# Stick-breaking q, k and half of v by seven-product block pairs, the residual spilled in the meantime, low parts of weights in the raw tile's bytes

## The chip, the cores and the metric

One Trainium2 chip, and one of its cores. The time is that of one execution on the device, in microseconds (us); the kernel before takes 2441.69 us (median of 3 runs, 2441.59 to 2443.45). The engines are TensorE (PE: matmuls, and PEld: its weight loads), VectorE (DVE), ScalarE (ACT), GpSimd (POOL) and SyncE (SP, whose queue issues the weight loads here).

## The reference

Two layers of a decoder over 256 positions of width 2048, in float32. Layer 0 runs state-space heads and latent attention side by side, layer 1 is stick-breaking attention; a SwiGLU FFN of width 5632 follows each. The part that the change is about:

```python
def stick_breaking_mixer(h, w_qkv, w_out):
    qkv = (h @ w_qkv).reshape(bsz, seq, 3, SB_HEADS, SB_HEAD_DIM)
    q, k, v = qkv[:, :, 0], qkv[:, :, 1], qkv[:, :, 2]
    for i in range(seq // Q_BLOCK):
        z = jnp.einsum('bqhd,bkhd->bhqk', q[:, q0:q1], k[:, :q1]).astype(jnp.float32) * scale
        log_keep = jnp.where(mask, -jax.nn.softplus(z), 0.0)
        later = lax.cumsum(log_keep, axis=log_keep.ndim - 1, reverse=True) - log_keep
        weight = jnp.where(mask, jnp.exp(jax.nn.log_sigmoid(z) + later), 0.0)
        outs.append(jnp.einsum('bhqk,bkhd->bqhd', weight.astype(v.dtype), v[:, :q1]))
    return jnp.concatenate(outs, axis=1).reshape(bsz, seq, SB_WIDTH) @ w_out

x = x + mix                                         # after each mixer
x = x + swiglu_ffn(rms_norm(x, ffn_norm[layer]), w_gate[layer], w_up[layer], w_down[layer])
```

There are 16 heads of 128; q, k and v have 2048 columns each.

## The kernel before

**Exact enough products.** A float32 weight tile (128 x 4 x 512, 1 MB, so 512 rows of the matrix by 512 columns) is loaded by SP's queue, cast by ACT to a rounded high part `wh` (line 271), and DVE subtracts it from the raw tile to get the low part `wl` (line 272). Activations are parted likewise. A product takes three matmuls of 512 columns for each 128 rows of K and each 128 positions: high by high, high by low, low by high.

**Two ways to project.** `project` (lines 371 to 373) does that for all 16 steps of K and both halves of the positions: 96 matmuls for one block of 512 columns. `pair` (line 585) does two blocks of 512 columns at once. Over the first 1024 rows of K it sees operand and weights as 2 x 2 blocks and computes the 2 x 2 product with seven block products (M1 to M7, 12 matmuls each) in place of eight; the second 1024 rows are done plainly (c0 to c3, 24 matmuls each): 180 matmuls. For that, DVE forms four differences of weight tiles (line 547; two into `wsum` tiles, one for M4, one over b12) and seven operand tiles (`operand_ready`). Four PSUM banks hold the sums. M1's, M5's, M6's and M7's state of a bank is copied by ACT as it stands after them (line 604, `kept`), and DVE adds the copy to another bank when that is done. `p2` and `p4` (the left block) are done with c2, `z` and `p3` (the right block) with c3. The tables `HALF` and `LATE` give the order of the eleven pieces; `LATE` is used for the first pair of an output projection, whose later operand blocks are not there yet.

**Where each is used.** Gate and up in both FFNs (22 pairs) and the three output projections (6 pairs) go by `pair`, all else by `project`, q, k and v of the stick layer among it.

**Stick layer** (`stick`). For each of four groups of four heads: project q, project k, scale both on leaving PSUM, transpose them on PE, then `stick_weights` (scores, mask on POOL, Abs and Exp on ACT for four heads; then Ln for four heads, the maximum step on DVE, a split; then the running sums by a triangular matmul and an Exp), then project v and `stick_out` (weights by v). The residual stays in the SBUF tile `xres` all along.

**What sets the order.** PE's order is the order of the code: tasks (`spawn`) advance at `tick`s, which stand every 4 to 8 matmuls. The other engines are in-order queues, which a scheduler fills by priority: weights (`wprio`) first, `urgent` ahead of them. Raw tiles have 4 buffers, `wh` and `wl` 3 each, `wsum` 2.

Of the kernel before, what the change touches and what calls it, by code (L numbers as in the profile page):

```python
# [8 lines left out]
F32 = mybir.dt.float32  # L9
# [17 lines left out]

class Trunk:
# [6 lines left out]
    def __init__(self, ctx, tc, ins, out):  # L35
# [4 lines left out]
        self.wp = ec(tc.tile_pool(name="weights", bufs=4))  # L40
# [4 lines left out]
        self.dp = ec(tc.tile_pool(name="scratch", bufs=1, space=bass.MemoryType.DRAM))  # L45
        self.shared = None
        self.region("acts")
        ctx.callback(self.region, None)
        self.banks = ["acc0", "acc1", "acc2", "acc3"]
        self.n = self.parts = 0  # L50
        self.pressing = []
        self.now, self.tasks = 0, []
# [23 lines left out]
    def after_urgent(self):  # L76
        order = ExitStack()
        for part, ins in self.pressing:
            if part <= self.parts - 3:
                order.enter_context(self.tc.issue_after(ins))  # L80
        self.pressing = [p for p in self.pressing if p[0] > self.parts - 3]
        return order
# [28 lines left out]
    def region(self, kind):  # L111

        if self.shared is not None:
            self.shared.__exit__(None, None, None)
        self.shared = None
        if kind:
            self.shared = self.tc.tile_pool(name=f"shared_{kind}", bufs=2, reuse_waits="tile")
            self.xp = self.shared.__enter__()

    def s2x(self, shape, dt=F32):  # L120

        return self.xp.tile([P, *shape], dt, name=self.nm("s2x"), tag="s2x", bufs=8)

    def wsum(self):
        return self.xp.tile([P, 4, 512], F32, name=self.nm("wsum"), tag="wsum", bufs=2)

    def wtile(self, tag="w", dt=F32, bufs=4):
        return self.wp.tile([P, 4, 512], dt, name=self.nm(tag), tag=tag, bufs=bufs)

    def part(self, tag):  # L130

        return self.wtile(tag, F32R, 3)
# [24 lines left out]
    FILL = 16  # L157


    def constants(self):  # L160
        nc, i = self.nc, self.i
        c = lambda shape, name, dt=F32: self.cp.tile(shape, dt, name=name)
        self.xres = c([P, 2, D], "xres")

        nc.gpsimd.memset(c([P, self.FILL], "fill"), 0.0)
# [103 lines left out]
    def split(self, hi, lo, src):  # L269
        nc = self.nc  # L270
        nc.scalar.copy(hi, src)  # L271
        return nc.vector.tensor_tensor(lo, src, hi.bitcast(F32), op=ALU.subtract).ins  # L272
# [57 lines left out]
    def load_split(self, view, nk, n):  # L330

        nc = self.nc
        for k0 in range(0, nk, 4):
            k1 = min(nk, k0 + 4)
            res = []
            with self.priority(self.wprio):
                self.wprio += 1000
                w = self.wtile()
                for dst, src in view(w, k0, k1):
                    nc.sync.dma_start(dst, src)  # L340
# [4 lines left out]
                wh, wl = self.part("wh"), self.part("wl")  # L345
                step = 1 if self.wprio < 102000 else 2 if self.wprio < 106000 else k1 - k0
                for c in range(0, k1 - k0, step):
                    d = c + step
                    self.last_split = self.split(wh[:, c:d, :n], wl[:, c:d, :n], w[:, c:d, :n])
                for k in range(k0, k1):  # L350
                    res.append((wh[:, k - k0, :n], wl[:, k - k0, :n]))
# [12 lines left out]
    def project(self, xT, view, nk, n=512, done=None, stagger=0):  # L364
# [4 lines left out]
        def unit(k, t, hi, lo, wh, wl):  # L369
            ts = slice(t * P, (t + 1) * P)  # L370
            nc.tensor.matmul(ps[t], hi[:, ts], wh, start=k == 0, stop=False)  # L371
            nc.tensor.matmul(ps[t], hi[:, ts], wl, start=False, stop=False)  # L372
# [31 lines left out]
    def norm_block(self, st, j, g, wait=2, rank=None):  # L404
# [3 lines left out]
        def gen():  # L408
            yield from self.transpose_split(
                lambda t, k: x[:, t, j * 512 + k * P:j * 512 + (k + 1) * P], res, g[:, 4 * j:4 * j + 4], wait, rank)  # L410
            for t in range(2):
                self.square_sum(x[:, t, j * 512:(j + 1) * 512], st["ssq"][:, t, j:j + 1])
        st["xT"].append((self.spawn(gen()), res))

# [19 lines left out]

    def add_tile(self, t, c, j, scale=None):
# [11 lines left out]
    def project_residual(self, st, view, scale=None, done=None):  # L447
# [3 lines left out]
        def add(n):  # L451
            def take(t, c, s):
                nc.vector.tensor_tensor(s, c, s, op=ALU.add)
# [74 lines left out]
    def wload(self, view, k0):  # L528
        w = self.wtile()
        with self.priority(self.wprio):  # L530
            self.wprio += 100
            for dst, src in view(w, k0, k0 + 4):
                self.nc.sync.dma_start(dst, src)
        return w

    def wsplit(self, w):
        wh, wl = self.part("wh"), self.part("wl")
        self.parts += 1
        with self.priority(self.wprio), self.after_urgent():
            self.wprio += 100  # L540
            self.last_split = self.split(wh, wl, w)
        return wh, wl

    def wsub(self, o, p, q):
        with self.priority(self.wprio):
            self.wprio += 100
            self.nc.vector.tensor_tensor(o, p, q, op=ALU.subtract)  # L547
# [3 lines left out]
    HALF = ("M1", "M5", "c0", "M3", "M6", "M2", "M7", "M4", "c1", "c2", "c3")  # L551

    LATE = ("M1", "M5", "M2", "M3", "M6", "M4", "M7", "c0", "c1", "c2", "c3")

    def pair(self, st, va, vb, left, right, order=HALF):
# [8 lines left out]
        for m in ("b11", "b12", "c0", "b22", "b21", "c1", "c2", "c3") if order is self.HALF else (  # L564
                "b11", "b12", "b22", "b21", "c0", "c1", "c2", "c3"):
            v = (va, vb)[int(m[2]) - 1 if m[0] == "b" else int(m[1]) % 2]
            raw[m] = self.wload(v, 4 * int(m[1]) - 4 if m[0] == "b" else 8 + int(m[1]) // 2 * 4)
        b11, b12, b22, b21 = (raw[m] for m in ("b11", "b12", "b22", "b21"))
        src = {"M1": b11, "M3": b22, "M2": b21, "M7": b12, **raw}
        t1, t2 = (self.wsum() for _ in range(2))  # L570
        src["M5"], src["M6"] = t1, t2
        self.join(st["xT"][0][0])
        self.join(st["xT"][1][0])
        if "paced" in st:
# [9 lines left out]
        def mm(b, x, y, stop=False):  # L584
            nc.tensor.matmul(ps[b], x, y, start=b not in started, stop=stop, skip_group_check=True)  # L585
            started.add(b)

        def add(b, x, w, keep=None):

            wh, wl = w  # L590
# [6 lines left out]
            for k, (hi, lo) in enumerate(x):  # L597
                mm(b, hi, wl[:, k], stop=k == n - 1)
# [15 lines left out]
        ops = lambda m: [(st["S"][place[m]][0][:, k], st["S"][place[m]][1][:, k]) for k in range(4)]  # L614
        for m in order:
            if m == "M1":
                self.wsub(t1, b12, b11)
            if m == order[2]:
                self.wsub(t2, b22, t1)
            if m == order[3]:  # L620
# [618 lines left out]
```

## Time and profile before

| | |
|---|---|
| median of 3 runs | 2441.69 us |
| the profiled execution | 2440.8 us, of which 2439.1 are the span |
| granted TensorE clock, mean | 0.999 |
| from HBM | 450.85 MB, 186 GB/s over the span |
| weight splits, wl from w (line 272) | 431, 966.8 us on DVE |
| casts, wh from w (line 271) | 431, 804.8 us on ACT |
| matmuls of `pair`, high and low parts | 3360 and 1680 |
| matmuls of `project`, each of three lines | 1600 |

The span runs from 0. The first layer's input projections end near 322 us, its output projections near 660, its FFN near 1338; q, k, v and the attention of the stick layer take from there to 1636; the second FFN starts near 1730. A row of a timeline or of the chain gives start and duration; a group gives instructions, busy time and mean ns of one, then the idle time ahead of them and what ended it.

### The profile page before, as it was taken

To read this page: it belongs to the slowest core of one execution; us is meant where nothing else is said; L and a number is where in the kernel's file an instruction comes from. 1 tells how busy PE (TensorE), PEld (TensorE's weight loads), DVE (VectorE), ACT (ScalarE), POOL (GpSimd) and SP (SyncE) were. 2 spreads that over 40 slices of the span, in tenths; PEclk is the share of its full clock that TensorE was granted. 3 is DMA by queue.
4 is the path that set the end of the run, shared out by engine and by line. 5 is a ranking of instruction groups with operands and counts; after the bars stand their busy time and mean duration, and the time that the engine had idled before them with its cause. 6 is when DMAs were issued, how large, how long until landed. Compare 5 with 4: busy or idle time off the path is not lost.

```text
span 2439.1 us, 27764 instructions
## 1 busy us (share of the span) xinstructions
PE 2406.7 (99%) x11104; PEld 1983.4 (81%) x11104; DVE 1815.6 (74%) x1533; ACT 1348.3 (55%) x1337; POOL 159.8 (7%) x210
## 2 busy tenths in 40 slices
PE   8999999999999999999999999999999999999998
PEld 7788888777788888888888888878788888888887
DVE  6776597578998777777775445559998777777775
ACT  6665565555755555555554556556665555555553
POOL 1341111110000000000000000000000000000001
PEclk9999999999999999999999999999999999999999
DMA  8654556424565666666665555545665566666663
GB/s 276 190 184 149 186 190 181 130 87 159 197 213 198 216 216 216 209 205 215 201 213 182 181 173 162 167 138 191 205 208 199 201 213 216 216 216 204 210 222 115
DMA packets 261377, 466.38 MB, mean 191 GB/s; under 512 B 21436, under 2 KB 46144, under 8 KB 261248
## 3 DMA queue, kind: packets, MB, share of 16 engines
q1 hardware_dynamic: 255168, 446.48, 55.1%
q0 software_dynamic: 5504, 17.09, 1.9%
q8 instruction: 87, 1.43, 0.2%
q10 hardware_dynamic: 576, 1.05, 0.1%
q14 instruction: 42, 0.34, 0.0%
HBM read 450.85 MB, written 2.13 MB: 186 GB/s over the span
## 4 chain that ended last, share of the span: by engine, by line
PE 77%; issue 14%; DVE 5%; ACT 2%; DMA 1%; POOL 1%; POOLq 0%; SPq 0%; DVEq 0%; ACTq 0%
PE acc L585 42%; PE acc L371 10%; PE acc L373 10%; PE acc L372 10%; DVE wl L272 2%; ACT wh L271 1%; DVE wsum L547 1%; DMA w<-in_w_out_even_dram 1%; PE at L1161 1%; POOL s L797 1%; PE at L1084 1%; PE tr L277 1%; PE at L1160 0%; PE tr L279 0%; DVE s L272 0%
## 5 line engine op out<-in xcount | busy, mean ns | idle before, releaser
L272 DVE TENSOR_TENSOR wl<-w,wh 128x2048 fp32r<-128x2048 f32 (+2 forms) x431 | 966.8, 2254 | 350.4 <-ACT wh L271 349.9
L271 ACT CAST wh<-w 128x2048 fp32r<-128x2048 f32 (+2 forms) x431 | 804.8, 1876 | 513.1 <-PE acc L373 244.8
L585 PE MATMUL acc<-wh,s 128*128 128x512 f32 x3360 | 838.2, 391 | 7.0 <-ACT wh L271 4.4
L585 PEld LDWEIGHTS acc<-wh,s 128*128 128x128 f32 x3360 | 627.1, 188 | 138.0 <-ACT wh L271 5.4
L371 PE MATMUL acc<-wh,s 128*128 128x512 f32 (+1 forms) x1600 | 639.2, 400 | 0.6 <-ACT wh L271 0.6
L373 PE MATMUL acc<-wh,s 128*128 128x512 f32 (+1 forms) x1600 | 621.7, 389 | 0.0
L372 PE MATMUL acc<-wl,s 128*128 128x512 f32 (+1 forms) x1600 | 620.4, 388 | 0.2 <-DVE wl L272 0.2
L585 PE MATMUL acc<-wl,s 128*128 128x512 f32 x1680 | 450.6, 390 | 4.6 <-DVE wl L272 4.6
L585 PEld LDWEIGHTS acc<-wl,s 128*128 128x128 f32 x1680 | 314.6, 188 | 73.8 <-DVE wl L272 8.7
L373 PEld LDWEIGHTS acc<-wh,s 128*128 128x128 f32 x1600 | 300.7, 188 | 63.3
L372 PEld LDWEIGHTS acc<-wl,s 128*128 128x128 f32 x1600 | 301.4, 188 | 58.0 <-issue 1.9
L371 PEld LDWEIGHTS acc<-wh,s 128*128 128x128 f32 x1600 | 301.1, 188 | 57.8 <-issue 1.9
L272 DVE TENSOR_TENSOR wl<-wsum,wh 128x2048 fp32r<-128x2048 f32 x84 | 192.0, 2287 | 43.8 <-ACT wh L271 42.7
L271 ACT CAST wh<-wsum 128x2048 fp32r<-128x2048 f32 x84 | 160.6, 1914 | 92.6 <-PE acc L373 60.3
L547 DVE TENSOR_TENSOR wsum<-w,wsum 128x2048 f32<-128x2048 f32 x56 | 129.1, 2306 | 4.7 <-DMA w<-in_w_out_even_dram 3.3
L604 ACT COPY s<-acc 128x512 f32<-128x512 f32 x112 | 65.8, 588 | 100.0 <-PE acc L585 100.0
L653 POOL DMA_DIRECT2D s<-s x44 | 23.7, 539 | 1471.4 <-DVE s L650 1405.8
L645 ACT ACTIVATE s<-s,rstd 128x512 f32<-128x512 f32 x44 | 31.9, 724 | 94.6 <-DVE s L644 94.6
L547 DVE TENSOR_TENSOR wsum<-w,w 128x2048 f32<-128x2048 f32 x28 | 65.0, 2320 | 24.0 <-DMA w<-in_w_up_dram 21.5
L547 DVE TENSOR_TENSOR w<-w,w 128x2048 f32<-128x2048 f32 x28 | 64.1, 2290 | 0.0
L326 ACT ACTIVATE s<-acc,rstd 128x512 f32<-128x512 f32 x48 | 32.2, 688 | 49.2 <-PE acc L373 47.9
L649 DVE TENSOR_TENSOR s<-acc,s 128x512 f32<-128x512 f32 x44 | 30.2, 687 | 36.5 <-PE acc L585 36.5
(230 smaller groups left out, 1281.3 us busy)
## 6 DMA issues: line engine op xcount, KB each, us to landing
w<-in_w_gate_dram SPq DMA_DIRECT2D x88, 1024.0 KB, 5.3
w<-in_w_up_dram SPq DMA_DIRECT2D x88, 1024.0 KB, 5.1
w<-in_w_down_dram SPq DMA_DIRECT2D x88, 1024.0 KB, 5.2
w<-in_w_qkv_dram SPq DMA_DIRECT2D x48, 1024.0 KB, 5.1
w<-in_w_in_dram SPq DMA_DIRECT2D x47, 1024.0 KB, 5.1
w<-in_w_out_even_dram SPq DMA_DIRECT2D x32, 1024.0 KB, 5.0
w<-in_w_out_odd_dram SPq DMA_DIRECT2D x16, 1024.0 KB, 4.9
s<-s POOLq DMA_DIRECT2D x44, 256.0 KB, 4.0
```

The source lines that it names most:

```text
L271: nc.scalar.copy(hi, src)
L272: return nc.vector.tensor_tensor(lo, src, hi.bitcast(F32), op=ALU.subtract).ins
L277: self.nc.tensor.transpose(out.bitcast(F32R), src, self.ident_r)
L326: self.nc.scalar.activation(o, ps[t], func, scale=scale[:, t:t + 1])
L371: nc.tensor.matmul(ps[t], hi[:, ts], wh, start=k == 0, stop=False)
L372: nc.tensor.matmul(ps[t], hi[:, ts], wl, start=False, stop=False)
L373: nc.tensor.matmul(ps[t], lo[:, ts], wh, start=False, stop=k == nk - 1)
L547: self.nc.vector.tensor_tensor(o, p, q, op=ALU.subtract)
L585: nc.tensor.matmul(ps[b], x, y, start=b not in started, stop=stop, skip_group_check=True)
L604: self.kept = nc.scalar.copy(o, ps[b]).ins
L645: nc.scalar.activation(s, s, AF.Silu, scale=rstd[:, t:t + 1])
L649: nc.vector.tensor_tensor(s, c, s, op=ALU.add)
```

## The change

**Stick layer.** For each group, q's and k's block of 512 columns become the two blocks of one `pair`; v of groups 0 and 1 is one more pair after group 1; v of groups 2 and 3 are two plain projections at the end. The first FFN now ends by making the operand sums for these pairs (`operand_sums`: 12 sums and 4 splits; M1, M2 and M4 take plain operands). The sums for the output projection are made late (`operand_late`). In `stick_weights` the splits are urgent and the triangular matmuls interleave with them.

**Memory.** `xres` is a fixed region now. It is written to DRAM by POOL's queue as the first FFN ends and comes back before the odd output projection; its bytes hold the scores `z` (`spare`) meanwhile. In layer 0 they hold the state-space head's `xdt`, and x is loaded anew before the even output projection. The low part is written over the raw tile: 6 slots that hold raw and low part, 2 for sums, 3 high parts and from the even output projection on 4. A load into a slot waits for the last matmul of the low part that was there.

**Orders.** `HALF` has M4 ahead of M7 and c2 ahead of c1; `LATE` has M3 and M6 ahead of M2. The difference for M4 is made at M6. Tiles are loaded three ahead, the others when their piece is reached.

```diff
-        self.wp = ec(tc.tile_pool(name="weights", bufs=4))
+        self.weight_slots()
+    HIGH, LOW, SUMS = 4, 6, 2
+    def wtile(self, tag="w"):
+        slot = min((s for s in self.slots[tag] if s.left == 0), key=lambda s: s.time)
+        slot.readers, slot.left = [], -1
+        return slot
+    def filled(self, slot, *writers):
+        if slot.last is not None:
+            for ins in writers:
+                self.tc.add_manual_dep(ins, slot.last.name, mybir.DependencyInfo(
+                    mybir.DependencyClass.Sync, mybir.DependencyReason.DATA), reason="the low part's last product")
...
-    def wsplit(self, w):
-        wh, wl = self.part("wh"), self.part("wl")
+    def wsplit(self, w, uses):
+        wh, wl = self.high(), w.part
...
-    HALF = ("M1", "M5", "c0", "M3", "M6", "M2", "M7", "M4", "c1", "c2", "c3")
-    LATE = ("M1", "M5", "M2", "M3", "M6", "M4", "M7", "c0", "c1", "c2", "c3")
+    HALF = ("M1", "M5", "c0", "M3", "M6", "M2", "M4", "M7", "c2", "c1", "c3")
+    LATE = ("M1", "M5", "M3", "M6", "M2", "M7", "M4", "c0", "c1", "c2", "c3")
...
-            if m == "M4":
+            if m == "M6":
+                load("b21")
+                b21 = src["M2"] = raw["b21"]
                 src["M4"] = self.wsum()
                 self.wsub(src["M4"], b21, t2)
...
-            self.norm_block(nst, n, gain_next)
+            self.norm_block(nst, n, gain_next, blocks=True, spill=self.saved, pause=4)
...
         for g in range(4):
-            qk = []
-            for part in range(2):
-                ps = self.project(xT, self.cols(wq, part * 2048 + g * 512), KD)
-                rstd = rstd or self.norm_end(st)
-                raw = self.evac(ps, AF.Copy, rstd)
+            raw = [[None, None], [None, None]]
+            self.pair(st, cols(0, g), cols(1, g), take(raw[0]), take(raw[1]))
+            qk, wts = [], []
+            for r in raw:
                 res = []
...
+            weights.append((self.spawn(self.stick_weights(qk, wts, g & 1)), wts))
+            if g in (0, 2):
+                continue
+            v = [[None, None], [None, None]]
+            if g == 3:
+                oT["late"] = self.spawn(self.operand_late(oT, 2))
+            if g == 3:
+                v = [self.evac(self.project(self.pairs(st["xT"]), cols(2, n), KD), AF.Copy, st["rstd"]) for n in (2, 3)]
+            else:
+                self.pair(st, cols(2, g - 1), cols(2, g), take(v[0]), take(v[1]))
...
+        oT["residual"] = self.spawn(self.residual_late(oT))
...
-            z, e = self.s2([N]), self.s2([N])
+            z, e = self.spare[4 * half + h][:, :N], self.s2([N])
...
+        self.slots["wh"] += self.more_high
         self.project_residual(uT, lambda n: self.cols(wo, n * 512), lambda: r_u)
```

**PE, the start of the stick layer.** Before, group 0's q projection takes high, low and high matmuls by turns for both halves of the positions (`acc_9921`, `acc_9922`), with the operand `s` and the weight parts `wh` and `wl`:

```order
L371 MATMUL acc_9921<-wh_9925,s_1675_9586 128x512
L372 MATMUL acc_9921<-wl_9926,s_1675_9586 128x512
L373 MATMUL acc_9921<-wh_9925,s_1676_9587 128x512
L371 MATMUL acc_9922<-wh_9925,s_1675_9586 128x512
L372 MATMUL acc_9922<-wl_9926,s_1675_9586 128x512
L373 MATMUL acc_9922<-wh_9925,s_1676_9587 128x512
```

Now the end of M1 (bank `acc_9160`), a transpose for the operand's third block, and the start of M5 (`acc_9161`). The low part is `w_69`, the raw tile's own bytes:

```order
L681 MATMUL acc_9160<-wh_66,s_875_8824 128x512
L681 MATMUL acc_9160<-wh_66,s_876_8825 128x512
L681 MATMUL acc_9160<-w_69,s_872_8807 128x512 x2
L681 MATMUL acc_9160<-w_69,s_875_8824 128x512 x2
L318 MATMUL tr_9179<-ident,xres 128x128 x4
L681 MATMUL acc_9161<-wh_67,s_897_8994 128x512
L681 MATMUL acc_9161<-wh_67,s_898_8995 128x512
```

In all, PE's order has 10,894 matmuls before and 10,834 now.

**PE, the first pair of the odd output projection, after M5.** Before, M5's low part in bank `acc_12073` is followed by a running sum of the attention (`at`) and by M2 in another bank, `acc_12074`:

```order
L585 MATMUL acc_12073<-wl_12103,s_1940_11178 128x512 x4
L816 MATMUL at_12118<-s_2082_11992,tri_l 128x384
L816 MATMUL at_12118<-s_2083_11993,tri_l 128x384
L818 MATMUL at_12118<-s_2082_11992,ones_r 128x128
L818 MATMUL at_12118<-s_2083_11993,ones_r 128x128
L585 MATMUL acc_12074<-wh_12128,s_1936_11158 128x512
```

Now M3 follows at once, in M5's bank `acc_11166`, whose state after M5 ACT has to copy:

```order
L681 MATMUL acc_11166<-wh_66,s_1090_10922 128x512
L681 MATMUL acc_11166<-wh_66,s_1091_10923 128x512
L681 MATMUL acc_11166<-wsum_81,s_1090_10922 128x512 x4
L681 MATMUL acc_11166<-wh_67,s_1096_10960 128x512
L681 MATMUL acc_11166<-wh_67,s_1097_10961 128x512
```

**ACT, group 0's attention.** Before, beside the projection of v: the last scores and Exps (lines 796 to 800), the table for Ln, the Ln of four heads (807), small casts of the sums for the triangular matmul, and a weight cast of the projection (`wh_10490`):

```order
L796 ACTIVATE s_1796_10337<-at_10334 128x384
L800 ACTIVATE s_1794_10321<-s_1794_10321 128x384
L799 ACTIVATE s_1797_10338<-s_1796_10337 128x384
L800 ACTIVATE s_1797_10338<-s_1797_10338 128x384
L807 ACT_TABLE_LOAD
L807 ACTIVATE s_1788_10287<-s_1788_10287 128x384
L807 ACTIVATE s_1791_10304<-s_1791_10304 128x384
L807 ACTIVATE s_1794_10321<-s_1794_10321 128x384
L271 CAST s_1801_10371<-s_1788_10287 128x384
L807 ACTIVATE s_1797_10338<-s_1797_10338 128x384
L271 CAST s_1803_10377<-s_1791_10304 128x384
L271 CAST wh_10490<-w_10488 128x2048
```

Now the attention of group 0 stands beside the pair of group 1's q and k. After the last Exp come the table, four Ln (line 950), the copy of bank `acc_9433` after M6 (702), a small cast, and M7's cast (`wh_68` from `w_76`):

```order
L943 ACTIVATE s_956_9566<-s_956_9566 128x384
L950 ACT_TABLE_LOAD
L950 ACTIVATE s_950_9517<-s_950_9517 128x384
L950 ACTIVATE s_952_9531<-s_952_9531 128x384
L950 ACTIVATE s_954_9549<-s_954_9549 128x384
L950 ACTIVATE s_956_9566<-s_956_9566 128x384
L702 COPY s_957_9605<-acc_9433 128x512
L305 CAST s_958_9627<-s_950_9517 128x384
L305 CAST wh_68<-w_76 128x2048
L305 CAST s_960_9645<-s_952_9531 128x384
```

In the pair of v's groups 0 and 1, and in that of group 3's q and k, M7's cast stands ahead of the last Exp and the table.

260 lines of the change are left out of this document (182 added, 78 removed).

## The prediction

> **What bounds the kernel now.** I read the page's engine table first, then the chain that ended last, then the waits of TensorE (PE), then the busy time by stage. The table's columns are busy time, share of the span and instructions.
>
> ```profile
> span 2439.1 us, 27764 instructions
> PE 2406.7 (99%) x11104; PEld 1983.4 (81%) x11104; DVE 1815.6 (74%) x1533; ACT 1348.3 (55%) x1337; POOL 159.8 (7%) x210
> 786.35 40.80 PE acc L585 x180
> ```
>
> PE stands still for only 32.4 us of the span. The third row, from the chain, is one pair of column blocks in the steady part of the first FFN: its 180 matmuls of 512 columns take 40.80 us, which is 0.2267 us each. A seven-product piece (12 matmuls) is therefore 2.72 us, a c piece (24) 5.44 us. The granted clock is 1.00 in all windows but the last, so this pitch may be used everywhere. Next the stages: here the columns are width, then busy time (and instructions) of PE, its weight loads, DVE, ACT and POOL, the clock, the DMA share and GB/s.
>
> ```profile
> 1270.00:1338.00 68.00, 68.00 (x318) 56.32 (x317) 40.17 (x36) 32.23 (x38) 1.08 (x2) 1.00 0.58 193
> 1338.00:1636.00 298.00, 298.00 (x1397) 249.05 (x1396) 157.50 (x137) 167.21 (x205) 16.93 (x16) 1.00 0.52 170
> 786.00:1230.00 444.00, 444.00 (x1992) 367.65 (x1991) 351.60 (x219) 230.94 (x162) 7.53 (x14) 1.00 0.61 207
> 600.00:720.00 120.00, 117.65 (x528) 96.08 (x527) 112.21 (x87) 78.42 (x73) 1.11 (x2) 1.00 0.62 207
> 1640.00:1800.00 160.00, 154.50 (x702) 126.32 (x701) 148.56 (x116) 104.91 (x104) 1.09 (x2) 1.00 0.55 188
> ```
>
> 1338 to 1636 is the projection of q, k and v with the stick attention. PE is busy for all 298 us and waits for nobody; DVE is busy for 157.5 us, 53%. So a matmul taken out here is a gain of its full pitch, as long as DVE and ACT keep up. Where DVE is at 79% (the steady FFN, 786 to 1230) PE still loses nothing. Where it is at 93% (600 to 720 and 1640 to 1800) PE loses 2.35 and 5.50 us, 2.8% of 280 us.
>
> **The matmuls that go.** PE's order counts 10,894 matmuls before and 10,834 after: 60 fewer, five pairs that do seven products where eight were done (12 matmuls each). 60 x 0.2267 = **-13.6 us**. Transposes and attention matmuls keep their number, and v's last two blocks stay plain.
>
> **What DVE and ACT get for it.** Rows of the page, with instructions, then busy time and mean ns.
>
> ```profile
> L272 DVE TENSOR_TENSOR wl<-wsum,wh 128x2048 fp32r<-128x2048 f32 x84 | 192.0, 2287 | 43.8 <-ACT wh L271 42.7
> L547 DVE TENSOR_TENSOR wsum<-w,wsum 128x2048 f32<-128x2048 f32 x56 | 129.1, 2306 | 4.7 <-DMA w<-in_w_out_even_dram 3.3
> L547 DVE TENSOR_TENSOR w<-w,w 128x2048 f32<-128x2048 f32 x28 | 64.1, 2290 | 0.0
> L649 DVE TENSOR_TENSOR s<-acc,s 128x512 f32<-128x512 f32 x44 | 30.2, 687 | 36.5 <-PE acc L585 36.5
> L271 ACT CAST wh<-wsum 128x2048 fp32r<-128x2048 f32 x84 | 160.6, 1914 | 92.6 <-PE acc L373 60.3
> L604 ACT COPY s<-acc 128x512 f32<-128x512 f32 x112 | 65.8, 588 | 100.0 <-PE acc L585 100.0
> ```
>
> Each new pair splits 11 tiles instead of 8 and forms 4 differences, so five pairs add 15 x 2.287 + 20 x 2.306 = 80.4 us on DVE, and 20 additions of a kept part 20 x 0.687 = 13.7 us. DVE rises to 157.5 + 94.1 = 251.6 of about 284 us, **88%**, between the two cases above. ACT gets 15 casts of 1.914 and 20 copies of 0.588, 40.5 us, and stands at 207.7 of 284, 73%. The third row is a difference written over its own input; it is no slower than the second, so I charge the low parts in the raw tile's bytes nothing. The operand sums at the end of the first FFN (12 sums of up to 512 columns and 4 splits, under 16 x 0.687 = 11 us) fall in 1270 to 1338, where DVE has 28 us free; without that cover they would cost up to 11 us.
>
> **The new waits, one by one.** (1) A load waits on SP's queue for the low part's last product of its slot, and later loads queue behind it. In a pair of the usual order, the slots for the next pair's first three tiles are free with the ends of M3, M2 and M7, 13.6, 19.0 and 24.5 us after its start; the pair lasts 40.8 us and a load lands 5.3 us after its issue (below), so I charge nothing. If a load came late, the differences behind it would pay.
>
> ```profile
> w<-in_w_gate_dram SPq DMA_DIRECT2D x88, 1024.0 KB, 5.3
> xres<-in_x_dram SPq DMA_DIRECT2D x4, 512.0 KB, 10.0
> ```
>
> (2) M4's difference overwrites the slot of M5's low part, so DVE waits until M5 has ended, 5.44 us into the pair; behind it stands M6's split, done at 5.44 + 2.31 + 2.29 = 10.0. PE wants it at 15.4 in the usual order (four pieces and eight matmuls), and in the LATE order at 10.0 plus the wait of (3). No charge. (3) In the LATE order M3 now follows M5 into the same bank, and M5's sum has to be copied first:
>
> ```profile
> 1790.60 1.75 PE L585 MATMUL acc<-wh,s 128*128 128x512 f32 x7
> 1790.80 0.59 ACT L604 COPY s<-acc 128x512 f32<-128x512 f32 x1 [1.71 <-PE acc L585]
> ```
>
> A copy after M1 begins 0.20 us after the next product starts and takes 0.59: 0.8 us in which PE now stands still, three times, **+2.4 us**. Bounds: 0 where PE would wait for its weights anyway, 3 x (0.8 + 1.9) = 8 where a cast of 1.9 us is in ACT's way. (4) The residual comes back from DRAM. Its last foreign readers stand before c0 and its first use after c2: 16.3 us for a load that took 10.0 above. No charge; were it late, DVE's addition and the next splits behind it would wait. The 12 added DMA issues on POOL's queue cost no more than that.
>
> **The attention beside a pair.** This is the place where I expect a new wait. In the pair that carries group 0's attention, ACT's order puts M7's cast behind the whole chain of four heads. Before, with one cast of weights in its midst as now, the chain went like this (time, duration):
>
> ```profile
> 1393.28 0.49 ACT L796 ACTIVATE s<-at 128x384 f32<-128x384 f32 x1 [1.01 <-PE at L794]
> 1404.38 1.28 ACT L807 ACT_TABLE_LOAD   x1
> 1405.67 1.35 ACT L807 ACTIVATE s<-s 128x384 f32<-128x384 f32 x3
> 1407.34 0.52 ACT L807 ACTIVATE s<-s 128x384 f32<-128x384 f32 x1
> ```
>
> From the first scores to the last logarithm: 14.6 us. Then come the copy of M6's sum (0.59), a small cast (0.5) and M7's cast (1.9), so M7's weights are ready 17.6 us after the first scores. Between these and M7, PE has half of c0 (2.7) and M3, M6, M2, M4 (10.9), with three more heads' scores at 0.56 each (from 1623.54 to 1624.10 below): 15.3 us. M7 waits 2.3 us, its low part some 0.5 more.
>
> ```profile
> 1623.54 0.59 PE L793 MATMUL at<-s,s 128*128 128x256 f32 x2
> 1624.10 0.47 PE L371 MATMUL acc<-wh,s 128*128 128x512 f32 x1
> ```
>
> In the two other pairs with attention M7's cast stands ahead of the logarithms; I put 1 us on each for scores and transposes that meet a busy DVE. Together **+5 us**. The least is 0 (the steady FFN's case); the most 2.8% of 284, which is 8, and the next rows decide how likely that is.
>
> ```profile
> 1470.79 0.41 POOL L797 TENSOR_SCALAR_AFFINE_SELECT s<-s 128x256 f32<-128x256 f32 x1 [1.02 <-ACT s L796]
> 1476.60 2.14 POOL L797 TENSOR_SCALAR_AFFINE_SELECT s<-s 128x256 f32<-128x256 f32 x1 [3.36 <-ACT s L796]
> 1476.18 2.29 DVE L272 TENSOR_TENSOR wl<-w,wh 128x2048 fp32r<-128x2048 f32 x1 [6.08 <-ACT wh L271]
> ```
>
> The same mask takes POOL 0.41 us while DVE is idle and 2.14 us beside a split, which ends at 1478.47, just before the mask does (1478.74). The chain has four masks, and DVE will be idle far less often. The Trainium skill says why, on the page "SBUF — State Buffer", section "SBUF: two separate sides": a DVE operation with two SBUF inputs and a GpSimd operation that reads SBUF lock each other out for a whole instruction. The trace agrees, with 0.41 and 2.14 us.
>
> **What the orders may give back.** Of the waits before, these are at pair starts (total us, times, longest):
>
> ```profile
> PE acc L585 <- DVE wl L272: 4.6, 7, 1.8
> PE acc L585 <- ACT wh L271: 4.4, 3, 2.2
> PE acc L585 <- DVE s L299: 2.6, 2, 1.8
> ```
>
> c2 ahead of c1 has the left half's sums ready 5.44 us earlier, so DVE's additions bunch less before the next pair; a fourth wh slot lets ACT and DVE work one piece further ahead; M4's difference is made earlier. That speaks to all 11.6 us. DVE's load at these places stays, so I take under half, **-5 us**; bounds 0 and -11.6.
>
> **Sum.** -13.6 + 2.4 + 5 - 5 = -11.2 us. The profiled execution took 2440.8 us (span 2439.1), 0.9 under the median of 2441.69; so 2429.6 for an execution like the profiled one, and **2430.5 us** as the median.
>
> **Rivals.** *Quiet stage, full return*: the chain hides and most of the pair-start waits go, -13.6 + 1 - 8 = -20.6 to -15 us, 2421 to 2426. For it: DVE at 79% cost PE nothing. Against: DVE at 88%. *DVE becomes the bound of the stick stage*: PE loses the 8 us that the 93% windows show, LATE 2.4, nothing is given back: -3.2 us, 2438.5. For it: 88% is nearer to 93 than to 79. *The masks wait for DVE*: if each of four masks takes 2.14 us in place of 0.41, the chain of 14.6 grows by 4 x 1.73 = 6.9 us, in full in the pair where M7's cast is behind it and by half, say, in the two others: 13.8 on top of the forecast, 2444, no change. It decides from masks that mostly meet a split; against it, DVE's own steps wait for the same logarithms, and DVE stands idle meanwhile. That the lock exists is what the page of the Trainium skill named above states. *Slower*: in each of the three pairs the four maximum steps and four splits of the heads queue behind a weight split as well, 8 x 2.29 = 18 us on the chain. Slower by 0.2% needs -13.6 + 2.4 - 5 + x = 4.9, so x = 21, 7 us in each pair: a chain of 14.6 + 7 - 2.8 = 18.8 us in all three, with M7's cast behind it. The full 18 us in each give 2441.69 - 16.2 + 54 = 2479. Against it: two of the three pairs have M7's cast ahead of the chain's end. *The change doesn't do what it says*: the order already shows 60 matmuls fewer, so no chance of its own.
>
> **How the numbers follow.** About 0.2% (4.9 us) is what a measurement of this kernel can tell from no change. The forecast (2426 to 2435): 0.63; the quiet stage (2421 to 2426): 0.15; DVE the bound (2435 to 2441): 0.13; the masks (2441 to 2447): 0.05; slower: 0.04. Faster, below 2436.8, takes the first two and 0.05 of the third: 0.83; within 0.2%: 0.08 + 0.05 = 0.13; slower: 0.04. The range, 2423 to 2438, leaves out 0.06 of the quiet case, 0.06 of the third, and the last two: 0.21.
>
> **What would show it.** Right: 60 matmuls fewer in PE's lines; DVE near 88% in the stick stage; M7's first matmul waiting 2 to 3 us for ACT beside group 0's attention; three waits near 0.8 us on ACT's copy; smaller waits at pair starts. Wrong: waits on ACT in all three attention pairs, masks over 2 us throughout, a load or the residual named as releaser, or steady FFN pairs longer than 40.80 us, since 22 of the 33 pairs are there and 0.5 us in each would undo the gain.

## The result, and the profile after

The changed kernel takes **2479.69 us** (median of 5 runs, 2479.17 to 2480.63), the kernel before beside it 2442.43 (5 runs, 2441.59 to 2444.80). The ratio is 1.0151, 95% interval 1.0136 to 1.0166: 37 us slower. The forecast was 2430.5 us, 11 us faster, with a range of 2423 to 2438. The time lies far outside it.

The page of the changed kernel, span and engine table (busy time, share, instructions):

```profile
span 2477.5 us, 27829 instructions
PE 2449.1 (99%) x11044; PEld 1973.9 (80%) x11044; DVE 1913.4 (77%) x1604; ACT 1387.9 (56%) x1376; POOL 158.9 (6%) x221
```

This is the row to start from. PE has 60 instructions fewer than before (11,104), as forecast, and yet is busy for 2449.1 us where it was busy for 2406.7: **42.4 us more work time for less work**. Its idle time went down, from 32.4 us to 2477.5 - 2449.1 = 28.4. So no wait explains the loss, and a search through the waits finds nothing. What is left is the time of one product. The chain of the changed kernel has the steady FFN pair that answers to the 40.80 us of before:

```profile
864.01 42.00 PE acc L681 x180
```

42.00 / 180 = 0.2333 us for a product in place of 0.2267. The prediction had named this sign ("steady FFN pairs longer than 40.80 us") and given it no case. The windows show the same over longer stretches (columns as in the prediction):

```profile
786.00:1230.00 444.00, 444.00 (x1935) 357.63 (x1934) 345.16 (x212) 226.79 (x158) 6.45 (x12) 1.00 0.60 201
1338.00:1636.00 298.00, 296.59 (x1360) 242.91 (x1359) 251.37 (x209) 210.57 (x254) 18.08 (x18) 1.00 0.55 180
```

In the first row's 444 us PE is busy throughout and the granted clock is 1.00 as before, but 1935 instructions get through instead of 1992. This stage runs none of the new pairs: its pairs were pairs before, though their pieces now come in the new order and their weights lie in the new slots. The second row is no such comparison, since the first pair of the stick layer begins only at 1367 us here and the row's first 29 us still belong to the first FFN. The groups of the page, for the products of the pairs and for their weight loads, first before (line, engine, operands, count, then busy us and mean ns, then idle time ahead):

```profile
L585 PE MATMUL acc<-wh,s 128*128 128x512 f32 x3360 | 838.2, 391 | 7.0 <-ACT wh L271 4.4
L585 PEld LDWEIGHTS acc<-wh,s 128*128 128x128 f32 x3360 | 627.1, 188 | 138.0 <-ACT wh L271 5.4
```

and after:

```profile
L681 PE MATMUL acc<-wh,s 128*128 128x512 f32 x3960 | 1018.4, 397 | 9.7 <-ACT s L702 4.2
L681 PEld LDWEIGHTS acc<-wh,s 128*128 128x128 f32 x3960 | 737.7, 188 | 187.4 <-ACT s L702 6.0
```

The load of the stationary operand (here the activations `s`, 128 x 128) takes 188 ns in both; the product that streams 512 columns of the weight tile past it is recorded 6 ns longer, 397 against 391. It is every product, in `project` as in `pair`, from the first ones on: the mean distance between the starts of two 512-column products that follow one another directly is 227.23 ns before (9,255 of them, those with a wait left out) and 233.28 ns after (9,221), and it is the same for high parts, low parts and low parts of differences (233.3 ns for each of the three in the pairs after).

Such a cost, the same everywhere in a program and nowhere in the code, points to what a change of memory pools moves without saying so: addresses. In the built programs (bytes within a partition):

```
                      before      after
weights begin          44032      17408
activations begin     125952     143168
distance               81920     125760  = 491 x 256 + 64
```

Weight tiles and activation tiles lie in their areas at multiples of 2048 bytes, and the slices that a product takes begin at multiples of 512 in a tile of activations and of 2048 in a tile of weights, so one number holds for all products. Before, the activations stand right behind ten weight tiles of 8192 bytes. After, 11,072 bytes of constants and small tiles (43 x 256 + 64) stand between.

### The profile page after: what moved, and what is told of

Same layout as the page of the kernel before. It is cut to its first block, busy times and chain, and to the rows that moved or that the text cites. A ratio compares the mean times of both kernels' runs of the same rounds, so it can differ in the third digit from the quotient of the medians.

```text
span 2477.5 us, 27829 instructions
## 1 busy us (share of the span) xinstructions
PE 2449.1 (99%) x11044; PEld 1973.9 (80%) x11044; DVE 1913.4 (77%) x1604; ACT 1387.9 (56%) x1376; POOL 158.9 (6%) x221
## 3 DMA queue, kind: packets, MB, share of 16 engines
q1 hardware_dynamic: 255168, 446.48, 54.5%
## 4 chain that ended last, share of the span: by engine, by line
PE 67%; issue 3%; DVE 1%; DMA 1%; ACT 0%; POOL 0%; POOLq 0%; DVEq 0%; ACTq 0%
PE acc L681 44%; PE acc L410 7%; PE acc L412 7%; PE acc L413 7%; PE tr L316 1%; DMA s<-s 0%; DVE w L311 0%; PE at L966 0%; DMA saved<-xres 0%; PE tr L351 0%; PE at L893 0%; PE at L936 0%; DMA w<-in_w_out_odd_dram 0%; DVE wsum L635 0%; POOL spare L940 0%
## 5 line engine op out<-in xcount | busy, mean ns | idle before, releaser
L311 DVE TENSOR_TENSOR w<-w,wh 128x2048 fp32r<-128x2048 f32 (+2 forms) x431 | 964.0, 2248 | 316.8 <-ACT wh L305 308.6
L681 PE MATMUL acc<-wh,s 128*128 128x512 f32 x3960 | 1018.4, 397 | 9.7 <-ACT s L702 4.2
L410 PE MATMUL acc<-wh,s 128*128 128x512 f32 (+1 forms) x1280 | 516.8, 404 | 0.6 <-ACT wh L305 0.6
L412 PE MATMUL acc<-w,s 128*128 128x512 f32 (+1 forms) x1280 | 502.4, 393 | 0.2 <-DVE w L311 0.2
L413 PE MATMUL acc<-wh,s 128*128 128x512 f32 (+1 forms) x1280 | 502.2, 392 | 0.0
L681 PE MATMUL acc<-w,s 128*128 128x512 f32 x1584 | 434.5, 396 | 0.2 <-DVE w L311 0.2
L681 PEld LDWEIGHTS acc<-w,s 128*128 128x128 f32 x1584 | 297.7, 188 | 72.9 <-DVE w L311 0.6
L412 PEld LDWEIGHTS acc<-w,s 128*128 128x128 f32 x1280 | 241.0, 188 | 53.2 <-issue 1.9
L305 ACT CAST wh<-wsum 128x2048 fp32r<-128x2048 f32 x99 | 189.3, 1912 | 87.1 <-PE acc L681 53.9
L311 DVE TENSOR_TENSOR wsum<-wsum,wh 128x2048 fp32r<-128x2048 f32 x99 | 226.7, 2289 | 4.0 <-ACT wh L305 4.0
L635 DVE TENSOR_TENSOR wsum<-w,wsum 128x2048 f32<-128x2048 f32 x66 | 151.1, 2289 | 39.9 <-PE acc L681 33.7
L681 PE MATMUL acc<-wsum,s 128*128 128x512 f32 x396 | 108.4, 395 | 0.0
L635 DVE TENSOR_TENSOR wsum<-w,w 128x2048 f32<-128x2048 f32 x33 | 76.6, 2322 | 41.0 <-DMA w<-in_w_up_dram 35.2
L681 PEld LDWEIGHTS acc<-wsum,s 128*128 128x128 f32 x396 | 74.3, 188 | 18.1
L635 DVE TENSOR_TENSOR w<-w,w 128x2048 f32<-128x2048 f32 x33 | 75.6, 2291 | 0.0
```

What stands on the lines that cost most here:

```text
L305: cast = nc.scalar.copy(hi, src).ins
L412: slot.used(nc.tensor.matmul(ps[t], hi[:, ts], wl, start=False, stop=False), self.clock)
L413: nc.tensor.matmul(ps[t], lo[:, ts], wh, start=False, stop=k == nk - 1)
L635: ins = self.nc.vector.tensor_tensor(o.raw, p.raw, q.raw, op=ALU.subtract).ins
L681: m = nc.tensor.matmul(ps[b], x, y, start=b not in started, stop=stop, skip_group_check=True)
```

## The experiments

The theories at this point. **A**: the pitch depends on the address of the stationary operand. **B**: the same with a coarser grain (512). **C**: the new slots cost it, by the low part written over its raw tile or by loads and differences that wait for single products. Later **R**: what counts is the distance between the two operands.

### Moving the activations, or the weights, by some bytes

Four kernels, beside the kernel before at 2442.66 us. The changed kernel with 64 unused bytes ahead of the activations:

```diff
+        ec(tc.tile_pool(name="pad", bufs=1)).tile([P, 16], F32, name="pad0", tag="pad")
         self.ap = ec(tc.tile_pool(name="acts", bufs=42))
```

> The changed kernel with one unused tile of 64 bytes per partition ahead of the pool of activations, so that its tiles, which every 128x512 product loads as its 128x128 stationary operand, begin at 143232 in place of 143168, a multiple of 128 bytes again as in the kernel before (125952). Nothing else moves. Theory A (TensorE's pitch depends on where the stationary operand begins, and 143168 is 64 bytes past a multiple of 128): the median distance between 128x512 products goes from 233 back to 227 ns, and about 9,490 x 6.05 ns = 57 us go from 2479.7, to 2420 to 2426. Theory B (it needs a multiple of 512, or the same place modulo 1024 as the weights): pitch 233, 2480. Theory C (the slots themselves: low part written over its raw tile, loads and differences that wait for single products): pitch 233, 2480.

The same line in the kernel before, between its weights and its activations:

> The kernel before with the same unused 64 bytes between its weights and its activations, which move from 125952 to 126016, 64 bytes past a multiple of 128; weights stay at 44032, the two weight sums move along by 64. Theory A: pitch from 227 to 233 ns for its 9,538 such products, + 57 us, 2495 to 2503. Theory B expects the same. Theory C: 2442, pitch 227.

In the kernel before, 64 bytes ahead of the weights and 448 behind them:

```diff
+        ec(tc.tile_pool(name="pada", bufs=1)).tile([P, 16], F32, name="pada0", tag="pada")
         self.wp = ec(tc.tile_pool(name="weights", bufs=4))
+        ec(tc.tile_pool(name="padb", bufs=1)).tile([P, 112], F32, name="padb0", tag="padb")
         self.ap = ec(tc.tile_pool(name="acts", bufs=42))
```

> The kernel before with 64 unused bytes ahead of the weights (the moving operand, 44032 to 44096) and 448 behind them, so that the activations stay at a multiple of 512 (126464). Theory A: only the stationary operand matters, pitch 227, 2442. Rival D, either operand off a multiple of 128 costs it: pitch 233, 2499. Theory B in the form of the same place for both operands: 233, 2499. Theory C: 2442.

In the kernel before, 32 bytes between weights and activations (8 words of padding in place of 16):

> The kernel before with 32 unused bytes between weights and activations (125984, 32 bytes past a multiple of 128). Theory A, if a row of 512 bytes is fetched in pieces that begin at a multiple of 64 or 128: at least what 64 bytes cost, pitch 233 or more, 2499 or more. If only the half of 128 matters: 227, 2442. Theory C: 2442.

Measured: 2475.83 us for the changed kernel with 64 bytes, 2492.14 (ratio 1.0199, 1.0184 to 1.0215) for the kernel before with 64, 2457.72 (1.0057, 1.0042 to 1.0072) with the weights moved, 2491.84 (1.0198, 1.0178 to 1.0219) with 32. The chain of the kernel before with 64 unused bytes:

```profile
861.17 42.00 PE acc L586 x180
```

That is the changed kernel's pair, to the hundredth of a microsecond, in a program that has nothing of the change: no slots, no low part in place, no waits on single products. **C falls.** A as I had it (a multiple of 128 is enough) falls too, since the changed kernel did not recover. And the kernel with the weights moved has a pitch of its own, which none of A, B and C allows, as its activations begin at a multiple of 512:

```profile
854.12 41.20 PE acc L587 x180
```

### What about the place counts

Four kernels, beside the kernel before at 2443.34 us. The changed kernel with both operands at multiples of 512:

```diff
+        ec(tc.tile_pool(name="pad", bufs=1)).tile([P, 48], F32, name="pad0", tag="pad")
         self.ap = ec(tc.tile_pool(name="acts", bufs=42))
...
-        base = -(-nc.sbuf_base // 1024) * 1024
-        nc.alloc_sbuf_tensor("arena", [P, n * 2048 + 4096], F32, align_bytes=1024)
+        base = -(-nc.sbuf_base // 512) * 512
+        nc.alloc_sbuf_tensor("arena", [P, n * 2048 + 4096], F32, align_bytes=512)
```

> The changed kernel with its arena of weights aligned to 512 instead of 1024 bytes (16896), and an unused tile of 192 bytes ahead of the activations, so that weights and activations both begin at a multiple of 512 (142848 for the activations). Nothing else differs. Theory B (a stationary row of 512 bytes must begin at a multiple of 512): pitch back to 227 ns, 2479.7 - 57 = 2420 to 2426, faster than the kernel before by about 20 us. Theory B2 (what counts is the activations' place modulo 1024, 0 before): 2475 to 2480, pitch 233. Theory C (slots and waits): 2475 to 2480.

The kernel before with 256 bytes between weights and activations:

> The kernel before with 256 unused bytes between weights and activations (126208, 256 past a multiple of 512). Theory B: pitch 233, 2492. Rival, a multiple of 256 is enough: pitch 227, 2442.

The kernel before with 64 bytes ahead of the weights only:

> The kernel before with 64 unused bytes ahead of the weights alone, so that weights (44096), activations (126016) and weight sums all move by 64 and keep their places relative to one another. Theory B, absolute places count: pitch 233 or a little more, 2492 to 2500. Theory R, the distance of the two operands modulo 512 counts: pitch 227, 2442.

The kernel before with 512 bytes between weights and activations:

> The kernel before with 512 unused bytes between weights and activations (126464, as in the run with the weights moved by 64, whose weights stood at 44096). Theory B: pitch 227, 2442, and then the 15 us of that run belong to the weights' 64 bytes. Theory B2 (activations modulo 1024): pitch 229, 2457, and then they belong to the activations' place.

Measured: 2428.54 us (ratio 0.9942, 0.9930 to 0.9955), 2443.20 (0.9999, 0.9990 to 1.0008), 2442.97 (1.0000, 0.9991 to 1.0009) and 2442.26 (0.9998, 0.9989 to 1.0007). The third decides between B and R. Its operands both begin 64 bytes past a multiple of 512, and its pair in the chain is that of the kernel before:

```profile
850.13 40.80 PE acc L586 x180
```

Neither address matters by itself; **the distance does** (R). The second says that 256 is as good as 512, where B had expected 2492. The fourth shares its activations' address with the kernel whose weights were moved, so that address does not explain that kernel's 15 us. And the first takes the loss away from the changed kernel: 2479.69 to 2428.54.

The last kernel of this kind tries a distance just short of a full turn: 32 bytes ahead of the weights and 480 behind them.

> The kernel before with 32 unused bytes ahead of the weights (44064) and 480 behind them (activations at 126464): the activations stand 224 modulo 256 behind the weights. So far, by this distance: 0 gave 227.2 ns, 32 and 64 233.3, 128 232.9, 192 229.1. If the cost falls with what is left up to 256: 228, 2445 to 2452. If every distance but 0 costs the same unless it is 192: 233, 2492.

It took 2491.57 us (1.0203, 1.0189 to 1.0217); the cost doesn't fall towards 256. All kernels so far and the version with activations first from below, by the distance between the begin of the stationary and of the moving operand modulo 256:

| distance mod 256 | kernels | steady pair, us | pitch, mean ns | against the kernel before |
|---|---|---|---|---|
| 0 | before; before with 64 ahead of both, with 256, with 512; changed with both at 512, with activations first | 40.80 | 227.2 | 0; changed - 15 and - 14 |
| 32 | before, 32 between | 42.00 | 233.2 | + 49 us |
| 64 | before, 64 between; changed | 42.00 | 233.3 | + 49 us; + 37 |
| 128 | changed, 64 between | 42.00 | 232.9 | + 33 |
| 192 | before, weights moved by 64 | 41.20 | 229.1 | + 15 |
| 224 | before, 32 and 480 | 42.00 | 233.2 | + 49 |

### The change with its operands in place

Without padding the same is had by entering the pool of activations ahead of constants and small tiles, so that it stands right behind the arena:

```diff
+        self.ap = ec(tc.tile_pool(name="acts", bufs=42))
         self.cp = ec(tc.tile_pool(name="const", bufs=1))
...
-        self.ap = ec(tc.tile_pool(name="acts", bufs=42))
```

> The changed kernel with the pool of activations entered ahead of the pools of constants and small tiles: it then stands right behind the arena of weights (132096), at a distance of a multiple of 256 bytes, with no padding and the arena as the change has it (17408). Theory R (the distance between the beginnings of the stationary and the moving operand, modulo 256, sets the pitch): 227 ns, 2425 to 2432 as with both at a multiple of 512. Theory P (something else of the padded version, such as the arena's 512, took part): another time, up to 2480.

2428.88 us against 2442.45 for the kernel before, ratio 0.9946 (0.9934 to 0.9959). This version beats both kernels, by 13.6 and by 50.8 us. Its page, and its pair in the chain:

```profile
span 2427.1 us, 27829 instructions
PE 2394.6 (99%) x11044; PEld 1975.7 (81%) x11044; DVE 1908.3 (79%) x1604; ACT 1388.2 (57%) x1376; POOL 160.7 (7%) x221
850.77 40.80 PE acc L681 x180
```

Against the changed kernel PE is busy 54.5 us less and idle 4.1 us more (32.5 against 28.4), 50.4 together, which is the difference of the spans. So the slower PE had hidden 4 us of waits. The pitch accounts for it: 6.05 ns at some 9,220 places are 55.8 us, against 54.5 measured.

On this base the change can be taken apart. First q, k and v by projections as before, so that only slots and orders are left (the operand sums at the end of the first FFN are left out too, nothing reads them):

```diff
-            self.pair(st, cols(0, g), cols(1, g), take(raw[0]), take(raw[1]))
+            for p in (0, 1):
+                ps = self.project(self.pairs(st["xT"]), cols(p, g), KD)
+                if "rstd" not in st:
+                    st["rstd"] = self.norm_end(st)
+                raw[p] = self.evac(ps, AF.Copy, st["rstd"])
...
-                self.pair(st, cols(2, g - 1), cols(2, g), take(v[0]), take(v[1]))
+                for p in (0, 1):
+                    v[p] = self.evac(self.project(self.pairs(st["xT"]), cols(2, p), KD), AF.Copy, st["rstd"])
...
-            self.norm_block(nst, n, gain_next, blocks=True, spill=self.saved, pause=4)
+            self.norm_block(nst, n, gain_next, spill=self.saved)
```

> The version with activations first, and q, k and v of the stick-breaking attention by projections as in the kernel before (10,862 products as there, no operand sums at the end of the first FFN). What is left of the change are the slots with the low part in the raw tile's bytes, the fourth wh slot, and the orders of the other 28 pairs. By the prediction's terms these are -5 + 2.4 us: 2440 against 2443 for the kernel before, and 8 to 14 us above the version with activations first. Rival, the slots cost time of their own: 2446 or more. Rival, the slots and orders give most of the gain: 2434 or less.

2440.98 us, ratio 0.9995 (0.9986 to 1.0004): slots and orders are worth nothing that this measurement can tell from 0, and the pairs in the stick layer 2440.98 - 2428.88 = 12.1 us. TensorE's products number 11,104 in this trace, as many as in the kernel before and 60 more than with the pairs.

Then the order for late operands, where the first matmul of M3 waits for the copy of M5's sum:

```diff
-    LATE = ("M1", "M5", "M3", "M6", "M2", "M7", "M4", "c0", "c1", "c2", "c3")
+    LATE = ("M1", "M5", "M6", "M3", "M2", "M7", "M4", "c0", "c1", "c2", "c3")
```

> The version with activations first, and M6 ahead of M3 in the order for late operands, so that M3 no longer follows M5 into the same bank (M6 takes the bank of M1, whose sum was copied beside M5). If the four waits for the copies (1.20, 1.83, 0.68 and 0.68 us in the padded version) are what that order costs, they go: 4.4 us less, 2422 to 2426. Rival: M6 needs one more load, a difference and a split before M3, and its weights come late instead: the time of the version with activations first, or more.

2434.69 us, 5.8 us slower than without this edit, where 2422 to 2426 were expected. TensorE's waits in this kernel (total us, times, longest):

```profile
PE acc L681 <- DVE wsum L311: 7.5, 3, 2.9
PE acc L681 <- ACT s L702: 0.7, 1, 0.7
```

The waits for copies are gone but for 0.7 us, and three waits for M6's low part, 7.5 us, stand in their place: the rival of the expectation. The timelines of DVE and of PE at the first of them (start, duration, idle time and its end in brackets):

```profile
330.36 2.29 DVE L311 TENSOR_TENSOR w<-w,wh 128x2048 fp32r<-128x2048 f32 x1 [4.12 <-ACT wh L305]
332.57 2.28 DVE L635 TENSOR_TENSOR wsum<-w,wsum 128x2048 f32<-128x2048 f32 x1
334.77 2.28 DVE L311 TENSOR_TENSOR wsum<-wsum,wh 128x2048 fp32r<-128x2048 f32 x1
...
337.11 1.20 PE L681 MATMUL acc<-wsum,s 128*128 128x512 f32 x4 [2.92 <-DVE wsum L311]
```

M4's difference (L635), made at M6 by this change, stands ahead of M6's low part on DVE, and M6 is now wanted one piece earlier than the 2.3 us of the difference allow.

The waits are only part of the 5.8 us. Between the two profiled executions PE's idle time grows by 3.0 us (2432.5 - 2397.0 = 35.5 against 32.5) and its busy time by 2.4. Part of the busy time is the granted clock, which falls behind the second of the three waits (it ends at 546.88 us; columns as before):

```profile
545.00:556.00 11.00, 9.19 (x28) 6.29 (x28) 7.71 (x9) 3.50 (x7) 0.00 (x0) 0.69 0.01 1
```

A clock of 0.69 over 11 us is 3.4 us of full speed lost here. The version with activations first loses as much, in two places of 1.7 us each (0.83 over the 10 us from 108 and from 340); this kernel has the one near 112 as well, 1.7 us more in all.

## Why the prediction was wrong

**The step that failed** is in its first part: "The granted clock is 1.00 in all windows but the last, so this pitch may be used everywhere." The pitch was read from the trace of before, where it is constant, and carried to the program after as if it belonged to the chip. It belonged to the placement of its operands. The 42.00 us of the changed kernel's pair, the same 42.00 us in the kernel before with 64 bytes in between, and 40.80 in the changed kernel without the distance of 64 show it from both sides. In the sum, 60 products go and all others keep their time: a term for them was put at nothing. The memory part of the change was looked at for waits, for what in-place writing does to DVE and for what the slots allow, never for where the tiles come to lie. None of the rivals had it: the slower case, 2479 us, came near the measured time by luck: it goes through DVE's queue in the attention pairs, and no such wait is in the trace. In the sum the missing term is + 50.8 us.

**The rest of the sum came out, in part by luck.** With the placement mended the kernel takes 2428.88 us, where 2430.5 were forecast. The mechanism of the gain was right, but several waits were not, and their errors cancel. The TensorE waits of that version, which the terms are read from:

```profile
PE acc L681 <- ACT s L702: 4.4, 4, 1.8
PE acc L681 <- DVE s L311: 3.2, 2, 2.5
...
PE acc L681 <- DVE s L338: 2.5, 2, 1.5
PE tr L316 <- DMA s<-s: 2.4, 2, 1.2
...
PE acc L681 <- ACT wh L305: 1.6, 1, 1.6
...
PE acc L681 <- DVE w L311: 0.2, 1, 0.2
```

- *60 products fewer, -13.6 us.* The two versions that differ by them, 12.1 us apart, have spans of 2427.1 and 2440.5 in their profiled executions. With M7's wait of 1.8 us (below) -13.6 makes -11.8.
- *DVE at 88%, ACT at 73% in the stick layer.* The window of 1340 to 1624 in the version with activations first, where its stick stage lies, below: 241.05 / 284 = 85% and 72%.
- *Waits of loads, of M4's difference, of the residual: 0.* None of them is a releaser of PE.
- *M3 behind M5, + 2.4 us (bounds 0 and 8).* Three waits of 1.2, 0.7 and 0.7 us, together 2.5: as forecast. The first row above has a fourth wait of 1.8 us, and that is another one: M7 of the first such pair enters M6's bank with only M2 in between, and M6's copy is late, because ACT stands behind a step of the norm (L289) that waits for DVE:

```profile
342.00 0.20 ACT L289 ACTIVATE rsy<-rsv 128x2 f32<-128x2 f32 x1 [2.39 <-DVE rsv L282]
342.11 0.57 ACT L702 COPY s<-acc 128x512 f32<-128x512 f32 x1
342.73 2.87 PE L681 MATMUL acc<-wh,s 128*128 128x512 f32 x8 [1.84 <-ACT s L702]
```

- *M7's cast beside group 0's attention, 2.3 + 0.5 us.* 1.6 for the cast, 0.2 for the low part. The 2 us put on the two other attention pairs did not come, so the term was 1.8 and not 5.
- *Waits at pair starts, -5 us out of 11.6.* Of the three rows of before, only the 2.6 us of the third are left, as 2.5 (the third row here); 3.2 us for DVE's low parts of the attention's output (the second row) are new, in c2 of one late pair and c0 of another. Net -5.9. But the prediction read the place of these waits wrongly. The first FFN begins near 634 us, not 660, so the waits at 660 and, in the second FFN, at 1754 are 26 to 27 us into a pair, at M4, as counting the pair's products shows:

```profile
1753.75 2.11 PE L585 MATMUL acc<-wh,s 128*128 128x512 f32 x8 [1.13 <-ACT wh L271]
```

M4's waits in pairs of the FFNs were 2.9 us of the 11.6, those in the pairs with the order for late operands 4.3, those of c0 2.6 and one of M5 1.8. All but c0's are gone. By their places, 7.2 of the 9.0 us that went speak for the earlier difference of M4 and the new late order rather than for c2 ahead of c1; no run takes these apart.
- *Not foreseen:* 2.4 us in which a transpose of the FFN's hidden rows waits for their DMA (the fourth row), twice. The trace of before has no such wait. What delays it was not tried.
- *Masks waiting for DVE.* The group on POOL before:

```profile
L797 POOL TENSOR_SCALAR_AFFINE_SELECT s<-s 128x256 f32<-128x256 f32 x16 | 16.9, 1058 | 339.1 <-ACT s L796 339.1
```

and in the version with activations first:

```profile
L940 POOL TENSOR_SCALAR_AFFINE_SELECT spare<-spare 128x256 f32<-128x256 f32 x16 | 17.9, 1123 | 233.9 <-ACT spare L939 233.9
```

The mean went from 1058 to 1123 ns (single masks take from 0.40 to 2.13 us, as they took from 0.41 to 2.14 before), not to 2.14 us: the rival had too high a rate. Added up, the terms as measured give -13.6 + 2.5 + 1.8 (M7 behind M6's copy) + 1.8 (M7's cast) - 5.9 + 2.4 (the DMA) = -11.0 us, where the forecast had -11.2. The median went down by 13.6 and the profiled span by 12.0; what is left between these is not put down to anything.

Of the same version here are the window of the stage, and from ACT's timeline the four logarithms with M7's cast behind them, as the prediction laid the chain out:

```profile
1340.00:1624.00 284.00, 282.21 (x1325) 235.81 (x1324) 241.05 (x192) 205.46 (x243) 18.59 (x17) 1.00 0.54 180
...
1405.67 1.77 ACT L950 ACTIVATE s<-s 128x384 f32<-128x384 f32 x4
1407.35 0.56 ACT L702 COPY s<-acc 128x512 f32<-128x512 f32 x1
1407.81 0.51 ACT L305 CAST s<-s 128x384 fp32r<-128x384 f32 x1
1408.22 1.90 ACT L305 CAST wh<-w 128x2048 fp32r<-128x2048 f32 x1
```

Copy, small cast and M7's cast follow the last logarithm in the order forecast, and PE is idle for 1.8 of 284 us, which is M7's wait.

So the gain of the change is that of its 60 products, and the waits that came and went cancel. PE's idle time is 2439.1 - 2406.7 = 32.4 us before and 32.5 after. The changed kernel lost this gain and 37 us more to 64 bytes.

## What to carry to other kernels

A TensorE that is 99% busy can still become slower without a single wait: divide a steady piece of the chain by its count, before and after, ahead of any search through the waits, and take a window whose products did not change as the control. A change that replaces memory pools moves every tile, so compare the begin of stationary and moving operands in the two built programs, here modulo 256 bytes, as carefully as the order of the instructions. An unused tile of 64 bytes in the good kernel is a test of that in one run, and the order in which pools are entered may be the whole cure.

## What the runs showed of the hardware

The time of a 128x512 float32r product whose stationary operand is loaded for it alone depends on where the two operands lie to one another in SBUF: 40.80 us for 180 of them at a distance of 0 modulo 256 bytes, 42.00 at 32, 64, 128 and 224, 41.20 at 192. Both operands may be 64 bytes off a multiple of 512 at no cost, if they are so together. Products of 256 weight columns do not show it: their median distance is 120 ns before and 118 ns with 64 bytes between. The transposes stay at 109 ns, but where their second operand lies to the first was not looked at. Distances between those tried were not measured, why 192 is cheaper than 64 or 224 was not tried, and what makes the distance matter is open; the runs show the dependence, not the mechanism.

The granted clock can fall to half for 3.4 or 6.8 us in the midst of a program. In these traces that happens 21 times, each time within 1.7 us of the end of a TensorE wait of 1.6 us or more, and 3.4 us of it cost 1.7 us. It does not follow every such wait: the profiled execution of the kernel before has one of 2.2 us (at 1644.55) and no fall before its end. Whether the wait sets it off was not tried; if it does, a wait can cost more than its length.

The Trainium skill's page "SBUF — State Buffer", section "Who interferes with whom", gives TensorE two read ports, one for the moving operand and one for the weight load, and calls them independent. By that rule 64 unused bytes would have left the kernel before at 2442.66 us; it took 2492.14, and here the measurement decides. The same page's section "Operand start alignment" asks only for a multiple of the element's size and says that this is about legality, not speed: the kernel with 32 bytes in between agrees that the two are apart, for such a start is legal there and the time is 2491.84 us.
